# The pooling pairs of a hybrid decoder layer, moved among the merge gate pairs and finished through DRAM

## The chip, the cores and the metric

The kernel runs on one core of one Trainium2 chip. The metric is the device time of one execution in microseconds; the median of several runs is compared. The traces come from the hardware profiler, one execution each.

## The reference

One layer over 1024 positions and 1024 channels. A modulated, normalised input h is projected by one wide matrix w_in. Three causal mixers work on parts of the projection, each is multiplied by its own SiLU gate and projected back, and the three are merged by sigmoid gates:

```python
proj = h @ w_in     # q, k, v, forget | q, k, v, low rank | pu | z_fox, z_gla, z_pool | merge
for g, w in enumerate((2, 4, 8, 16)):            # pooling, 128 channels per group
    lo, hi = g * 128, (g + 1) * 128
    mean = (csum[lo:hi] - lagged_by_w[lo:hi]) / min(count, w)
    diff = mean - pu[..., lo:hi]
    o_pool[..., lo:hi] = (diff @ w_pool[g]) * pool_scale[lo:hi]
y_pool = (o_pool * silu(z_pool)) @ w_br_pool      # y_fox, y_gla alike
merged = sigmoid(m_fox) * y_fox + sigmoid(m_gla) * y_gla + sigmoid(m_pool) * y_pool
out = x + gate * rms_norm(merged @ w_out)
```

All of it is in 32-bit floats.

## The kernel before

Matmuls run on operands split in a high and a low part of a faster float format (`split`, L109: ScalarE writes the high part, VectorE subtracts it for the low part, L110 and L112), three matmuls for one product (`mm3`, L143).

The work goes in stages: start and normalisation, the linear attention (GLA), then the projections for everything else, then the forgetting attention (FoX), the branch projections and the output. The change lies in the stage of projections. There, 256 columns of w_in make one *pair* (`pair`, L900) of two 128-channel output tiles over 1024 positions. `seven` (L843) computes a pair with seven products of 12 matmuls, after Strassen and Winograd. The operands made of h stay in SBUF (`h_combos`, L786, makes the combinations once, on GpSimd and VectorE). The operands made of weights are formed for each pair by `load_seven` (L812): two loads of 512 KB, four additions on GpSimd (S tiles, L825), seven splits. Their tiles rotate over nine slots (`wt`), so a pair's weights can be at most nine products ahead.

PSUM has eight banks under five names; the seven products take them as `("acc", "a", "c", "a", "c", "b", "d")`, with one bank each behind b and d and two behind the others. The sums of products (u, v, p and the outputs, L858, L868, L882) are read out by VectorE, ScalarE and GpSimd with priority. The first output tile of a pair (`small_out`, L947) takes a slot of tag `wh`, which has three, and the second a slot of `wl`, also three. The second of each pair's weight loads takes `wh` too, so that it reuses the slot that the first output tile of the pair two before it has left. When an output half is complete, `fn` runs on it (`silu2`, `tanh_m`), and when both are, `fin` takes the tile on: stored by `to_dram`, or split and stored as two parts by `parts_to_dram` (L930). Two tiles of 1024 columns rotate under `big` (L926), one slot each; the running sums, the high parts and the tiles of `og_parts` (L940, the GLA output times its gate, read back from DRAM) go through these two.

The order in the program is: gate pairs zg0 and zg1, with h_combos between them, then for q = 0, 1 the pairs pu, zp (the pooling input and its gate), fq, fk, zf (FoX queries, keys and gate), then twelve merge gate pairs m, the first four each followed by one `og_parts`, and in the twelfth the first loads and scores of FoX (`start_ahead`). For pooling, `window` (L963) makes the running sums of a group by doubling (one to four steps for widths 2 to 16) and turns the tile of pu into the differences. Both groups' windows stand behind the pair pu, and `fin_pool` stands in the gate pair zp: it splits the differences into parts dh and dl, multiplies them by the group's w_pool in banks b and d (tiles pspl), scales the product by pool_scale and by the gate (L990), splits and stores. For the first group of a pair that comes ahead of the pair's seventh product in the program, for which bank d is needed.

This order isn't that of the chip: a planner with a simulated clock (`schedule_with_timeline_sim=True`) places each engine's instructions, and each SP-issued transfer, by readiness and program order; slots and banks are given out in program order. Each engine and the SP queue then run their list in order, and a wait holds what stands behind it.

Of the kernel before, what the change touches and what calls it, by code (L numbers as in the profile page):

```python
# [29 lines left out]
def kernel(  # L30
# [42 lines left out]
    def halves():  # L73
        return ((0, slice(0, HALF)), (1, slice(HALF, S)))
# [7 lines left out]
    def bank(tag, name, shape=(P, HALF)):  # L82
        if tag == "acc":
            return ps_acc.tile(list(shape), F32, tag="acc", name=name, bufs=2)
        return ps_acc.tile(list(shape), F32, tag=tag, name=name, bufs=BANKS[tag])
# [3 lines left out]
    def spill(name, n):  # L89
        return [dram.tile([P, S], F32, tag=f"{name}{j}", name=f"{name}{j}") for j in range(n)]  # L90
# [5 lines left out]
    fqh_dram, fkh_dram = spill("fqh_d", 4), spill("fkh_d", 4)  # L96
    fql_dram, fkl_dram = spill("fql_d", 4), spill("fkl_d", 4)
    sz_dram, szg_dram, m_dram = spill("sz_d", 4), spill("szg_d", 4), spill("m_d", 24)
    gate_dram = dram.tile([8, P], F32, tag="gate_d", name="gate_d")
    ff_dram = dram.tile([8, S], F32, tag="ff_d", name="ff_d")  # L100
    fc_dram = dram.tile([8, S], F32, tag="fc_d", name="fc_d")
# [7 lines left out]
    def split(raw, hi, lo, scale=1.0, E=None):  # L109
        i = A.activation(hi, raw, AF.Copy, scale=scale)  # L110
        if scale == 1.0:
            j = (E or V).tensor_tensor(out=lo, in0=raw, in1=hi.bitcast(F32), op=ALU.subtract)  # L112
        else:
            j = V.scalar_tensor_tensor(  # L114
                out=lo, in0=raw, scalar=scale, in1=hi.bitcast(F32), op0=ALU.mult, op1=ALU.subtract
            )
        return i, j
# [25 lines left out]
    def mm3(ps, wh, wl, rh, rl, first, last):  # L143
        T.matmul(ps, wh, rh, start=first, stop=False)  # L144
        T.matmul(ps, wh, rl, start=False, stop=False)  # L145
        T.matmul(ps, wl, rh, start=False, stop=last)  # L146
# [753 lines left out]
    def pair(col, name, f, fin, fn=None):  # L900

        o, done = {}, {}

        def dst(j):
            o[j] = big(f"o{j}_{name}") if f is plain else small_out(j, name)
            return o[j]

        def post(j, i, hs):
            if fn is not None:
                with tc.high_priority():  # L910
                    fn(o[j][:, hs], f"{name}{j}{i}")
            done[j] = done.get(j, 0) + 1
            if done[j] == 2:
                fin(j, o[j])

        f(col, name, dst, post)
        return o
# [3 lines left out]
    def to_dram(tiles):  # L921
        return lambda j, t: stores.append(nc.sync.dma_start(tiles[j], t))
# [3 lines left out]
    def big(name, dt=F32):  # L926
        brot[0] += 1
        return sh(GT[brot[0] % 2], name, dt=dt)

    def parts_to_dram(t, hi_d, lo_d, name, scale=1.0, hi=None):  # L930
        if hi is None:
            hi = big(f"hi_{name}", F32R)
        split(t, hi, t.bitcast(F32R), scale)
        nc.sync.dma_start(hi_d, hi.bitcast(F32))
        nc.sync.dma_start(lo_d, t)
# [38 lines left out]
        V.scalar_tensor_tensor(out=u[:, w - 1 : S], in0=cur[:, w - 1 : S], scalar=1.0 / w, in1=u[:, w - 1 : S],  # L974
                               op0=ALU.mult, op1=ALU.subtract)

    def fin_pool(q, d):
        def f(j, t):
            g = 2 * q + j
            raw = cst.tile([P, P], F32, tag="Fd", name=f"wpr{g}", bufs=2)  # L980
            nc.sync.dma_start(raw, w_pool[0, g])
            wph = sp.tile([P, P], F32R, tag="wph", name=f"wph{g}")
            wpl = sp.tile([P, P], F32R, tag="wpl", name=f"wpl{g}")
            split(raw, wph, wpl)
            dh, dl = big(f"dh{g}", F32R), big(f"dl{g}", F32R)
            split(d[j], dh, dl)
            for i, hs in halves():
                ps = bank("bd"[i], f"pspl{g}{i}")
                mm3(ps, wph, wpl, dh[:, hs], dl[:, hs], True, True)
                V.scalar_tensor_tensor(out=t[:, hs], in0=ps, scalar=psc[:, g : g + 1], in1=t[:, hs],  # L990
                                       op0=ALU.mult, op1=ALU.mult)
            parts_to_dram(t, oph_dram[g], opl_dram[g], f"op{g}")
        return f

    pair(C_ZG, "zg0", plain, to_dram(szg_dram[0:2]), silu2)
    h_combos()
    pair(C_ZG + 256, "zg1", seven, to_dram(szg_dram[2:4]), silu2)
    for q in range(2):
        u = pair(C_PU + q * 256, f"pu{q}", seven, lambda j, t: None)
        for j in range(2):  # L1000
            window(2 * q + j, u[j])
        pair(C_ZP + q * 256, f"zp{q}", seven, fin_pool(q, u), silu2)
        pair(C_FQ + q * 256, f"fq{q}", seven, fin_qk(q, fqh_dram, fql_dram, SCL, "q"))
        pair(C_FK + q * 256, f"fk{q}", seven, fin_qk(q, fkh_dram, fkl_dram, 1.0, "k"))
        pair(C_ZF + q * 256, f"zf{q}", seven, to_dram(sz_dram[2 * q : 2 * q + 2]), silu2)
    vf = {}
    hq = {}
    kk = {}
# [77 lines left out]
    def start_ahead():  # L1086
        load_qk(0)
        for i in (7, 6):
            ahead[0, 0, i] = scores(0, 0, i)

    for q in range(12):
        if q == 11:
            hook[0] = start_ahead
            wrot[0] = 3
        pair(C_M + q * 256, f"m{q}", seven, to_dram(m_dram[2 * q : 2 * q + 2]), tanh_m)
        if q < 4:
            og_parts(q)

    tr_stack.close()
    tq_stack.close()  # L1100
# [245 lines left out]
```

## Time and profile before

| what | value |
|---|---|
| runs | 1119.51, 1112.82, 1114.29 us |
| median | 1114.29 us |
| the profiled execution | 1110.77 us, span 1109.0 us, mean granted clock 0.992 |
| stage of the pairs zg1 to zf1 | about 302 to 521 us of the span |
| merge gate pairs | about 521 to 752 us |

The profile counts from the span's start. PE is TensorE's matmuls, PEld its weight loads, DVE VectorE, ACT ScalarE, POOL GpSimd, SP the engine that issues nearly all transfers. A window's row has the stretch, its length, each engine's busy time with its instructions in brackets, TensorE's granted clock as a share of full speed, the busy share of the DMA engines, and GB/s. A row of the timeline has start, duration, engine, line, operation, output and inputs, and in square brackets the idle time before with what ended it.

### The profile page before, as it was taken

What the parts mean: (1) busy time and instruction counts of PE and PEld (TensorE: products, weight loads), DVE (VectorE), ACT (ScalarE), POOL (GpSimd) and SP (SyncE); (2) the same over time, 40 slices, a digit from 0 to 9 for tenths busy, and PEclk for the clock granted to TensorE, in tenths of its full rate; (3) what the DMA queues carried; (4) which work ended last, traced back from release to release, by engine and by line L of the source; (5) the groups of instructions that cost most, each with busy time, mean ns of one, the idle gap of its engine ahead of it and who ended that gap; (6) DMA issues with size and microseconds to landing.
All of it is one profiled execution on the core that took longest, in us unless ns stands there. A gap on an engine that the chain in (4) does not pass through costs nothing.

```text
span 1109.0 us, 15436 instructions
## 1 busy us (share of the span) xinstructions
PE 1058.1 (95%) x5599; PEld 855.0 (77%) x5599; DVE 741.7 (67%) x1403; ACT 462.6 (42%) x877; POOL 384.8 (35%) x339
## 2 busy tenths in 40 slices
PE   5899989999998999899999999999999999999997
PEld 3579779887776888688888888887776776787886
DVE  6638796674898777997656565557675769487323
ACT  6336453443643342343434344435543437343111
POOL 1023152123266145445555444431210434353000
PEclk9999999999999999999999999999999999999999
DMA  9930111202141543156763333359959562464232
GB/s 316 310 106 20 39 40 59 81 25 67 72 128 50 184 142 95 38 198 221 254 200 114 116 124 121 125 154 349 271 184 286 206 173 86 169 221 132 84 106 77
DMA packets 97776, 159.33 MB, mean 144 GB/s; under 512 B 8266, under 2 KB 71324, under 8 KB 97700
## 3 DMA queue, kind: packets, MB, share of 16 engines
q1 hardware_dynamic: 97348, 157.54, 44.5%
q8 instruction: 44, 0.72, 0.3%
q10 hardware_dynamic: 352, 0.80, 0.3%
q14 instruction: 32, 0.26, 0.1%
HBM read 113.16 MB, written 45.16 MB: 143 GB/s over the span
## 4 chain that ended last, share of the span: by engine, by line
PE 68%; DMA 12%; DVE 11%; issue 3%; POOL 3%; ACT 2%; SPq 1%; DVEq 0%; ACTq 0%; POOLq 0%
PE pp_m L146 7%; PE pp_m L144 7%; PE pp_m L145 7%; PE pso L1298 3%; PE pso L1297 3%; PE po L1156 3%; PE pso L1296 3%; PE psy L144 2%; PE psc L655 2%; PE psy L146 2%; PE psy L145 2%; PE tp L1146 2%; DMA kl<-fkl_d 2%; DMA wa<-in_w_ada_dram 1%; PE ps_gv L168 1%
## 5 line engine op out<-in xcount | busy, mean ns | idle before, releaser
L144 PE MATMUL psy<-ogh,wh_y 128*128 128x512 f32 x192 | 75.9, 401 | 6.7 <-DMA ogh<-ogh_d 3.7
L146 PE MATMUL psy<-ogh,wl_y 128*128 128x512 f32 x192 | 74.0, 394 | 1.8 <-DVE wl_y L114 1.8
L145 PE MATMUL psy<-ogl,wh_y 128*128 128x512 f32 x192 | 75.5, 393 | 0.0
L144 PE MATMUL pp_m<-hh,w_m 128*128 128x512 f32 x192 | 74.7, 389 | 0.0
L145 PE MATMUL pp_m<-hl,w_m 128*128 128x512 f32 x192 | 74.7, 389 | 0.0
L146 PE MATMUL pp_m<-hh,w_m 128*128 128x512 f32 x192 | 74.7, 389 | 0.0
L112 DVE TENSOR_TENSOR w_m<-wr_m,w_m 128x512 fp32r<-128x512 f32 x36 | 43.1, 1201 | 44.1 <-ACT w_m L110 44.1
L1052 POOL TENSOR_SCALAR_AFFINE_SELECT Fd<-F 128x128 f32<-128x128 f32 x64 | 22.1, 350 | 127.7 <-DVE mx L1074 89.2
L1081 ACT ACTIVATE t<-t,ng 128x1024 f32<-128x1024 f32 (+3 forms) x64 | 49.6, 776 | 37.3 <-DVE ng L1079 34.7
L112 DVE TENSOR_TENSOR w_m<-S_m,w_m 128x512 fp32r<-128x512 f32 x48 | 57.2, 1221 | 3.1 <-ACT w_m L110 2.3
L566 POOL TENSOR_TENSOR e<-cum 128x256 f32<-128x256 f32 x24 | 17.8, 743 | 108.6 <-DVE kt L570 45.6
L1069 DVE CUSTOM_DVE_ANT_0 t<-psL,F 128x512 f32<-128x512 f32 (+2 forms) x80 | 41.3, 524 | 20.7 <-PE psL L1066 9.0
L793 POOL TENSOR_TENSOR sb<-hh,hl 128x512 f32<-128x512 f32 x16 | 23.1, 1467 | 85.4 <-PE pr L330 65.9
L1297 PE MATMUL pso<-wol,mh 128*128 128x512 f32 (+1 forms) x136 | 51.2, 377 | 0.0
L1296 PE MATMUL pso<-woh,mh 128*128 128x512 f32 (+1 forms) x136 | 51.2, 376 | 0.0
L957 ACT ACTIVATE o_m<-o_m 128x512 f32<-128x512 f32 x48 | 29.0, 628 | 53.1 <-DVE o_m L858 31.7
L1298 PE MATMUL pso<-woh,ml 128*128 128x512 f32 (+1 forms) x136 | 51.0, 376 | 0.0
L1300 DVE TENSOR_TENSOR yo<-pso,gb 128x512 f32<-128x512 f32 (+1 forms) x17 | 11.2, 660 | 55.8 <-ACT jk L1299 55.8
L144 PEld LDWEIGHTS psy<-ogh,wh_y 128*128 128x128 f32 x192 | 36.3, 189 | 15.4 <-DMA ogh<-ogh_d 4.0
L1148 ACT COPY PT<-tp 128x512 f32<-128x512 f32 (+1 forms) x64 | 31.6, 504 | 38.5 <-PE tp L1146 35.3
L1146 PE MATMUL tp<-ident,t 128*128 128x128 f32 x288 | 45.4, 280 | 1.9 <-ACT t L1081 1.1
L1156 PE MATMUL po<-PT,vf 128*64 128x256 f32 (+1 forms) x320 | 45.6, 366 | 0.0
(585 smaller groups left out, 3334.8 us busy)
## 6 DMA issues: line engine op xcount, KB each, us to landing
wa<-in_w_ada_dram SPq DMA_DIRECT2D x24, 512.0 KB, 8.3
wr_m<-in_w_in_dram SPq DMA_DIRECT2D x24, 512.0 KB, 3.7
m_d<-o_m SPq DMA_DIRECT2D x24, 512.0 KB, 2.9
m_in<-m_d SPq DMA_DIRECT2D x24, 512.0 KB, 6.5
xn<-in_x_dram SPq DMA_DIRECT2D x8, 512.0 KB, 6.3
kl<-fkl_d SPq DMA_DIRECT2D x16, 256.0 KB, 9.3
kk<-fkh_d SPq DMA_DIRECT2D x16, 256.0 KB, 10.7
F<-fc_d SPq DMA_DIRECT2D x8, 512.0 KB
```

Source lines behind the costliest of these rows:

```text
L112: j = (E or V).tensor_tensor(out=lo, in0=raw, in1=hi.bitcast(F32), op=ALU.subtract)
L144: T.matmul(ps, wh, rh, start=first, stop=False)
L145: T.matmul(ps, wh, rl, start=False, stop=False)
L146: T.matmul(ps, wl, rh, start=False, stop=last)
L1069: V.tensor_tensor_reduce(out=t[:, c0:e], in0=ps[:, : e - c0], in1=Fb[p, h][:, c0:e], scale=1.0, scalar=-3e38, op0=ALU.subtract, op1=ALU.ma ...
L1081: A.activation(t[:, :W], t[:, :W], AF.Exp, bias=ng[:, 0:1], accum_out=sm)
L1146: T.transpose(tp[:, j, :], t[:, kb * P : (kb + 1) * P], ident)
L1148: A.copy(pts[h, kg][:, 0:nb, qs], tp[:, 0:nb, :])
L1156: T.matmul(po[64 * h : 64 * h + 64, q0:256], vf[p // 2, kb // 4][:, kb % 4, col : col + 64], pts[h, kb // 4][:, kb % 4, q0:256], start=(kb ...
L1296: T.matmul(ps[:, :w], mh[k][:, sl], hi, start=(k == 0), stop=False)
L1297: T.matmul(ps[:, :w], mh[k][:, sl], lo, start=False, stop=False)
L1298: T.matmul(ps[:, :w], ml[k][:, sl], hi, start=False, stop=(k == NK - 1))
```

## The change

The four pooling pairs leave their places ahead of the q pairs. They now stand one by one ahead of the first four merge pairs: pu0, m0, zp0, m1, pu1, m2, zp1, m3. The window of a pair's first group runs when its output tile is complete, the second group's after the following merge pair; the differences are stored to DRAM (`df_dram`). The gate pairs store their SiLU tile (`szp_dram`). The finishing of a group (`pool_parts`) reads both back behind the merge pairs 4 to 7, one group each, in the two rotating tiles, and takes the banks acc and b in place of b and d.

```diff
+    df_dram, szp_dram = spill("df_d", 4), spill("szp_d", 4)
...
-    def fin_pool(q, d):
+    def fin_window(q, late):
         def f(j, t):
             g = 2 * q + j
-            raw = cst.tile([P, P], F32, tag="Fd", name=f"wpr{g}", bufs=2)
-            nc.sync.dma_start(raw, w_pool[0, g])
-            wph = sp.tile([P, P], F32R, tag="wph", name=f"wph{g}")
-            wpl = sp.tile([P, P], F32R, tag="wpl", name=f"wpl{g}")
-            split(raw, wph, wpl)
-            dh, dl = big(f"dh{g}", F32R), big(f"dl{g}", F32R)
-            split(d[j], dh, dl)
-            for i, hs in halves():
-                ps = bank("bd"[i], f"pspl{g}{i}")
-                mm3(ps, wph, wpl, dh[:, hs], dl[:, hs], True, True)
-                V.scalar_tensor_tensor(out=t[:, hs], in0=ps, scalar=psc[:, g : g + 1], in1=t[:, hs],
-                                       op0=ALU.mult, op1=ALU.mult)
-            parts_to_dram(t, oph_dram[g], opl_dram[g], f"op{g}")
+            def run():
+                window(g, t)
+                nc.sync.dma_start(df_dram[g], t)
+            if j == 0:
+                run()
+            else:
+                late.append(run)
         return f
+    def pool_parts(g):
+        raw = cst.tile([P, P], F32, tag="Fd", name=f"wpr{g}", bufs=2)
+        nc.sync.dma_start(raw, w_pool[0, g])
+        wph = sp.tile([P, P], F32R, tag="wph", name=f"wph{g}")
+        wpl = sp.tile([P, P], F32R, tag="wpl", name=f"wpl{g}")
+        split(raw, wph, wpl)
+        d, dh = big(f"d{g}"), big(f"dh{g}", F32R)
+        nc.sync.dma_start(d, df_dram[g])
+        dl = d.bitcast(F32R)
+        split(d, dh, dl)
+        pss = []
+        for i, hs in halves():
+            ps = bank(("acc", "b")[i], f"pspl{g}{i}")
+            mm3(ps, wph, wpl, dh[:, hs], dl[:, hs], True, True)
+            pss.append(ps)
+        t = big(f"zp{g}")
+        nc.sync.dma_start(t, szp_dram[g])
+        for (i, hs), ps in zip(halves(), pss):
+            V.scalar_tensor_tensor(out=t[:, hs], in0=ps, scalar=psc[:, g : g + 1], in1=t[:, hs],
+                                   op0=ALU.mult, op1=ALU.mult)
+        parts_to_dram(t, oph_dram[g], opl_dram[g], f"op{g}")
...
     for q in range(2):
-        u = pair(C_PU + q * 256, f"pu{q}", seven, lambda j, t: None)
-        for j in range(2):
-            window(2 * q + j, u[j])
-        pair(C_ZP + q * 256, f"zp{q}", seven, fin_pool(q, u), silu2)
         pair(C_FQ + q * 256, f"fq{q}", seven, fin_qk(q, fqh_dram, fql_dram, SCL, "q"))
...
+    def pool_pair(q, kind, late):
+        if kind == "u":
+            pair(C_PU + q * 256, f"pu{q}", seven, fin_window(q, late))
+        else:
+            pair(C_ZP + q * 256, f"zp{q}", seven, to_dram(szp_dram[2 * q : 2 * q + 2]), silu2)
...
+    late = []
     for q in range(12):
+        if q < 4:
+            pool_pair(q // 2, "uz"[q % 2], late)
         if q == 11:
             hook[0] = start_ahead
             wrot[0] = 3
         pair(C_M + q * 256, f"m{q}", seven, to_dram(m_dram[2 * q : 2 * q + 2]), tanh_m)
+        if late:
+            late.pop()()
         if q < 4:
             og_parts(q)
+        elif q < 8:
+            pool_parts(q - 4)
```

## Rows read from the trace of the kernel before

**Rows 1.** The page, part 1: busy time, share of the span, instructions.

```profile
PE 1058.1 (95%) x5599; PEld 855.0 (77%) x5599; DVE 741.7 (67%) x1403; ACT 462.6 (42%) x877; POOL 384.8 (35%) x339
```

**Rows 2.** Windows of the two stages: PE, PEld, DVE, ACT, POOL, clock, DMA, GB/s.

```profile
302.00:345.00 43.00, 42.33 (x186) 34.37 (x185) 42.67 (x46) 15.30 (x27) 29.81 (x18) 1.00 0.36 112
345.00:360.00 15.00, 9.95 (x42) 7.29 (x41) 11.79 (x16) 7.36 (x14) 9.03 (x6) 1.00 0.13 36
...
462.00:480.00 18.00, 17.07 (x68) 13.98 (x69) 15.06 (x19) 8.02 (x14) 6.98 (x6) 0.91 0.37 118
480.00:521.00 41.00, 41.00 (x183) 33.94 (x182) 33.03 (x35) 16.68 (x24) 20.23 (x12) 1.00 0.59 205
521.00:736.00 215.00, 214.99 (x948) 177.41 (x947) 133.81 (x143) 89.02 (x152) 113.86 (x72) 1.00 0.46 151
```

**Rows 3.** Windows of PE alone: pooling stage, merge pairs.

```profile
302.00:520.90 218.90, 207.94 (x895) 0.98 0.39 128
520.90:731.00 210.10, 210.09 (x926) 1.00 0.45 148
```

**Rows 4.** Waits of PE, 282 to 521: us in total, times, longest.

```profile
PE pp_zp L144 <- DVE o_zp L990: 3.9, 1, 3.9
PE pspl L144 <- DVE o_zp L858: 3.3, 2, 2.6
PE pspl L144 <- ACT dh L110: 2.5, 1, 2.5
...
PE pspl L145 <- DVE dl L112: 0.5, 1, 0.5
...
PE pp_zg L146 <- DVE w_zg L112: 0.4, 1, 0.4
PE pp_pu L146 <- DVE w_pu L112: 0.3, 1, 0.3
```

**Rows 5.** Windows of 4 us around the two holes, columns as in rows 2.

```profile
358.00:362.00 4.00, 2.21 (x7) 1.80 (x8) 3.56 (x6) 1.79 (x4) 1.91 (x2) 0.82 0.05 16
362.00:366.00 4.00, 4.00 (x15) 3.20 (x14) 3.08 (x4) 1.75 (x4) 0.00 (x0) 0.75 0.91 306
...
460.00:464.00 4.00, 1.38 (x5) 0.88 (x4) 4.00 (x6) 1.72 (x3) 3.48 (x2) 0.87 0.00 0
464.00:468.00 4.00, 4.00 (x14) 3.20 (x13) 3.85 (x7) 0.01 (x1) 0.00 (x0) 0.70 0.37 100
```

**Rows 6.** Window of the instructions on the running sums, DVE alone.

```profile
302.00:521.00 219.00, 31.25 (x32) 0.98 0.39 128
```

**Rows 7.** Timeline of DVE: first sum and last difference of width 8.

```profile
437.50 2.31 DVE L969 TENSOR_TENSOR win<-o_pu 128x1023 f32<-128x1023 f32 x1
...
446.69 1.21 DVE L974 SCALAR_TENSOR_TENSOR o_pu<-win,o_pu 128x1017 f32<-128x1017 f32 x1
```

**Rows 8.** DMA issues: KB each, median us to landing.

```profile
m_d<-o_m SPq DMA_DIRECT2D x24, 512.0 KB, 2.9
...
opl_d<-o_zp SPq DMA_DIRECT2D x4, 512.0 KB, 4.8
```

**Rows 9.** The two parts of the differences: ns min, median, max; first, last start.

```profile
L110 ACT ACTIVATE dh<-o_pu x4: 1044/1050/1062, 342.8 to 470.0; 128x1024 fp32r<-128x1024 f32 x4
L112 DVE TENSOR_TENSOR dl<-o_pu,dh x4: 1210/1222/1227, 344.7 to 478.0; 128x1024 fp32r<-128x1024 f32 x4
```

**Rows 10.** Groups of DVE, 302 to 521: the scaled pooling products.

```profile
L990 DVE SCALAR_TENSOR_TENSOR o_zp<-pspl,colv,o_zp 128x512 f32<-128x512 f32 x8 | 5.7, 748 | 0.6 <-PE pspl L146 0.2
```

**Rows 11.** Timeline of SP: a load of queries for the attention.

```profile
568.68 0.52 SPq L1027 DMA_DIRECT2D hq<-fqh_d  x1
```

**Rows 12.** Timeline of PE's weight loads, 598 to 606.

```profile
603.33 0.19 PEld L146 LDWEIGHTS pp_m<-T2h,w_m 128*128 128x128 f32 x1 [0.33 <-DVE w_m L112]
```

**Rows 13.** Waits of SP's queue, 282 to 755.

```profile
SPq L816 <- DVE dl L112: 20.3, 1, 20.3
```

## The prediction

> **What bounds the kernel now.** I read the busy shares first: PE 95% of the span [rows 1], so a change can gain where PE isn't full, or where its clock is low. The windows come next, cut at the stages. In the merge gate pairs PE is busy 214.99 of 215 us, with DVE at 133.81 [rows 2]: that stretch is bound by PE alone. In the stage before it, which holds the pooling pairs, PE is full in the last 41 us but has holes at 345 to 360 (9.95 of 15 us) and in 462 to 480, while DVE is busy 42.67 of 43 us just ahead of the first hole [rows 2]. So the pooling work overloads DVE, and PE pays for it shortly after.
>
> How much it pays is best counted in matmuls. In the merge pairs 926 of them take 210.1 us, 0.2269 us each; in the pooling stage 895 take 218.9 us [rows 3]. At 0.2269 they would take 203.1, so 15.8 us are lost there. That loss has three parts. Idle PE is 218.9 - 207.94 = 11.0 us [rows 3]. The list of PE's waits says who ended it: the product that waits for a PSUM bank held by a pooling product 3.9, the pooling products for that bank 3.3, for the high part of the differences 2.5, for their low part 0.5, together 10.2; what is left, 0.4 and 0.3, are weights of the pairs around it [rows 4]. Next, the granted clock: behind the two holes it reads 0.82 and 0.75, then 0.87 and 0.70 over 4 us each [rows 5], that is part of the time at the lower of the two levels, 1.2 instead of 2.4 GHz. The missing shares, (0.18 + 0.25 + 0.13 + 0.30) x 4, are 3.4 us of full-speed work. The rest, 1.4 us, are slow first matmuls after each stop.
>
> **The change, part by part.** No matmul is added or dropped: seven products per pair and the 24 pooling matmuls stay. So on PE the sum is only about waits.
>
> Removed: the pooling pairs leave the stretch in which the work of h_combos and of the first gates is still queued on DVE. All of the 15.8 us can go, except the 0.7 of weights at the start, where a pair of q takes the place of a pooling pair and needs its weights just as early. That is -15.1. What was next behind the removed waits is PE itself, as in 480 to 521 [rows 2], where the same q, k and gate pairs run with no hole at 33.03 of 41 us on DVE.
>
> Moved, windows: the running sums and differences cost DVE 31.25 us in 32 instructions [rows 6]. They now fall among eight pairs of 84 x 0.2269 = 19.06 us. A merge pair costs DVE 133.81 / 215 x 19.06 = 11.9 us, so eight of them and the windows want 126 of 152 us, 83%, and some more with the gates' products. The cover is there, but not idle: DVE was about as full as that in 480 to 521, without a PE hole. I cost this at nothing. If the cover fails, the place is this: the first half's tile of a pooling pair stays occupied until the window is done and stored, and the second weight load of the pair after next takes that same slot. The window of width 8 ran from 437.50 to 447.90 [rows 7], begun 3 us after its pair's products ended, and a store lands in 4.8 us at worst [rows 8]: 18 us after the pair, of the 19 that the merge pair between gives. Then load, splitting and subtraction come late by up to 3 us, once for each of two pairs. Bounds 0 to 6, taken 0, because without the neighbouring window of width 16 behind it DVE is less crowded there.
>
> Added, the way through DRAM: eight stores and eight reloads of 512 KB, 8.4 MB, on the same queue. The merge stretch moves 151 GB/s at a DMA share of 0.46; q and k pairs at 205 GB/s and 0.59 had no PE hole [rows 2]. 8.4 MB over eleven pairs, 210 us, add 40 GB/s. I cost bandwidth at nothing. The price is in latency, which I follow for one group: reload of the differences 4.8 (the slowest shown), high part 1.05, low part 1.22 [rows 9], six matmuls 1.36, reload of the gate 4.8, two scaled products 1.5 [rows 10], high and low part again 2.3, store 4.8 [rows 8]: 21.8 us. The two rotating tiles make the four groups a chain, since the next reload takes the slot that the last store leaves. 21.8 against 19.06 per pair means that the groups fall behind by 2.7 us each, four groups some 11 us, and there are four more merge pairs behind them: late, but not at the end of the stage. With the quickest shown, 2.9 us per transfer [rows 8], the chain is 16.1 us and keeps up. The Trainium skill ("DMA: Bandwidth & Descriptors", section "Anatomy of one DMA — SWDGE (gpsimd) path") gives about 2.0 us plus bytes over 436 GB/s, measured on another kind of queue; 512 KB would be 3.2 us, an estimate, and the chain 17.0, which also keeps up and leaves the sum as it is.
>
> Added, waits on PE: the pooling products stand in PE's order where the planner guessed their operands ready, and the matmuls of the next pair stand behind. Today's waits for the two parts, 2.5 and 0.5, stay in kind, so I take 3.0 us for the four groups. The lower bound is 0: the planner can place them late, behind other work. Even less isn't excluded, if they fill gaps of weights; but there are hardly any gaps (0.01 us in 215). The upper bound is the longest wait of today, 3.9, for each of four groups: 15.6. I stay near the low end because the two waits over a bank lose their reason. The scaled product no longer needs the gate's own pair to be through silu; that gate lies in DRAM by then. Bank d isn't used any more, and bank b is free again after matmuls, reload and products, 1.36 + 4.8 + 1.5 = 7.7 us, against 13 us until the next pair's sixth product wants it.
>
> Added, waits on other queues: the gate's reload waits on SP until the pooling matmuls have let its tile go, with the next weight loads behind it; and the scaled product waits on DVE for that reload, with weight splits behind it. Both are the last rival's matter; in the sum they are nothing as long as the planner keeps the order.
>
> The sum: -15.8 + 0.7 + 3.0 = -12.1 against the profiled 1110.77, 1098.7 us. The median of the shown runs lies 3.5 above the profiled one, so I expect 1102.
>
> **The rivals.** *All of it comes back.* The pooling products find their operands ready and PE never waits: -15.1 or a little more, 1099. For it: the merge pairs ran through the multiplication of the linear attention's gate, a chain of the same kind through DRAM, without a single wait, and the planner moves loads far ahead (loads of q for the attention stand at 568.68, long before their pair [rows 11]). Against it: the four pooling products are the very place where PE waited.
>
> *The stall moves along.* DVE at 83% on average is full in bursts, and splits for weights and for differences stand in one queue. Then the 10.2 us of waits recur with their clock and restarts, 4.8, and nothing is left: -15.1 + 15 = 0, 1114. For it: weights in the merge pairs come just in time, one weight load into PE waited 0.33 us for a split on DVE [rows 12]. Against: today the bursts come on top of h_combos' leftovers, afterwards they don't.
>
> *A reload blocks the weights: slower.* A load of weights has stood behind a wait on SP for 20.3 us here, until DVE had made a low part [rows 13]. After the change each of the four gate reloads waits on SP for its pooling matmuls, and since the weights have no slack [rows 12], what SP loses PE loses soon after. It decides from 15.1 / 4 = 3.8 us per group; at 8 us, about the time the bank is held, it costs 32, so +17: 1131. The Trainium skill states as a rule of DMAs, on the same page and section, that "any semaphore wait happens on the issuing sequencer before dispatch"; by that rule this happens whenever the planner's order is wrong by more than the slack, and the 20.3 us agree with it. Against: the order is planned with the same waits in it, and today's fill of SP with waiting stores, in 480 to 521, cost PE nothing.
>
> *The change doesn't do what it says.* The planner issues by readiness, not by place in the program. If it pulls the finishing of groups forward to the last pooling pairs, it lands where the windows load DVE most, some 5 us of waits: 1105.
>
> **How the numbers follow.** Forecast (1099.5 to 1107) 0.45; all back 0.22; the stall moves along 0.22; slower 0.08; not as said 0.03. One per cent of 1114.29 is 11.1 us, about what a measurement of this kernel can tell from no change, so faster begins at 1103.1. The forecast lies astride it, somewhat over half on the fast side: 0.28 + 0.22 make 0.50 for faster. Same takes 0.17 + 0.21 + 0.03 = 0.41, slower 0.09. The range: down to 1096, which is all back on a run 2 us below the median; up to 1114, which holds the pooling waits' upper bound, -15.1 + 15.6. Outside lie the blocked reloads, part of the stall that moves along, and little below, under 2 in 10.
>
> **What would show it.** The stage of q, k and gates from 302 on without a PE hole and with clock 1.00; no wait of a pooling product or of a seventh product for a scaled product; in the merge stretch PE waits of the pooling products of about 3 us in all, for high or low parts; SP's waits over the weights not longer than now. I am wrong if PE's list of waits names weights or their loads in the merge pairs (windows or SP too late), if the granted clock falls there, or if DVE is found full while PE waits.

## The result and the profile after

The forecast was 1102 us, 1096 to 1114. The changed kernel took 1126.45 us in the median of four runs (1124.15 to 1133.44), beside 1115.53 for the kernel before: a ratio of 1.0103, 95% interval 1.007 to 1.0137. Run again later on another occasion (e15 below) the ratio was 1.0096 (1.0066 to 1.0126). So it is slower by 1%, some 11 us, and outside the range on the slow side. The profiled execution took 1126.96 us, 16.2 more than the profiled one of before. Up to line 97 the numbers of both kernels agree; L109 to L112 of before are L110 to L113 now, L143 to L146 are L144 to L147, `load_seven`'s L816 is L817, the sums' L858 is L859.

The busy shares first; they answer to [rows 1]. PE is busy 10.7 us longer with the same 5599 matmuls, which already says that part of the loss is clock and not idle time.

```profile
PE 1068.8 (95%) x5599; PEld 862.4 (77%) x5599; DVE 748.3 (67%) x1403; ACT 463.3 (41%) x877; POOL 389.1 (35%) x339
```

The windows of after, columns as in [rows 2]. The q, k and gate pairs now end near 440, the merge pairs with the pooling pairs among them follow.

```profile
345.00:360.00 15.00, 15.00 (x68) 12.43 (x67) 12.04 (x12) 6.69 (x11) 9.17 (x6) 1.00 0.41 149
...
460.00:480.00 20.00, 17.51 (x75) 13.38 (x74) 14.24 (x15) 6.75 (x12) 12.13 (x7) 1.00 0.48 160
480.00:500.00 20.00, 14.93 (x55) 10.97 (x54) 13.06 (x13) 7.40 (x13) 10.65 (x6) 0.88 0.68 236
500.00:520.00 20.00, 20.00 (x78) 16.23 (x77) 14.93 (x19) 8.23 (x15) 7.50 (x6) 0.86 0.33 106
...
580.00:600.00 20.00, 16.66 (x69) 13.01 (x68) 13.47 (x15) 6.98 (x11) 8.45 (x5) 0.94 0.47 166
600.00:640.00 40.00, 37.46 (x155) 29.96 (x154) 25.99 (x28) 17.03 (x30) 21.05 (x14) 0.94 0.43 146
640.00:660.00 20.00, 16.56 (x61) 13.11 (x61) 13.05 (x17) 8.63 (x14) 8.42 (x6) 0.83 0.52 173
660.00:768.00 108.00, 108.00 (x480) 89.48 (x479) 69.56 (x89) 43.59 (x73) 45.73 (x33) 1.00 0.57 178
```

The hole of before at 345 to 360 is closed: 15.00 of 15 us. New holes lie at 460 to 500 and 580 to 660; from 480 to 520 and from 580 to 660 the clock reads 0.83 to 0.94. The same in matmuls, as for [rows 3], with PE alone:

```profile
302.00:440.00 138.00, 137.31 (x605) 1.00 0.42 143
440.00:767.80 327.80, 310.92 (x1314) 0.96 0.49 162
```

At 0.2269 us, 605 matmuls need 137.3 us: up to 440 only 0.7 us are lost, as much as the weights that the prediction left in. The 1314 behind need 298.1 of 327.8 us, so 29.7 us are lost: 16.9 idle (327.8 - 310.92), and 12.8 in busy time that is longer than at full clock. Who ended the idle time, as in [rows 4], for 282 to 770:

```profile
PE pp_m L145 <- ACT w_m L111: 5.6, 2, 3.3
PE pspl L145 <- ACT dh L111: 3.4, 1, 3.4
PE pp_m L147 <- DVE w_m L113: 2.8, 2, 2.5
PE pspl L145 <- DVE o_m L859: 2.4, 1, 2.4
PE pp_zp L145 <- ACT w_zp L111: 1.9, 1, 1.9
...
PE pp_zp L147 <- DVE w_zp L113: 0.5, 1, 0.5
```

Weights (w_m, w_zp) make 10.8 us, pooling products (pspl) 5.8. The weights come first, so the next view is the list of SP, which loads them. First the timeline of SP at the first two holes (PE stood still before 468.28 and before 491.15), then its waits in 455 to 492, as in [rows 13]:

```profile
457.99 0.34 SPq L985 DMA_DIRECT2D df_d<-o_pu  x1
460.56 0.34 SPq L943 DMA_DIRECT2D og_in<-og_d  x1
461.01 0.67 SPq L817 DMA_DIRECT2D wr_zp<-in_w_in_dram  x1
...
481.04 0.32 SPq L936 DMA_DIRECT2D ogl_d<-szg  x1
481.45 0.41 SPq L943 DMA_DIRECT2D og_in<-og_d  x1
...
484.27 0.32 SPq L944 DMA_DIRECT2D szg<-szg_d  x1
484.69 0.43 SPq L817 DMA_DIRECT2D wr_m<-in_w_in_dram  x1
```

```profile
SPq L985 <- DVE win L969: 10.8, 1, 10.8
SPq L817 <- POOL S_zp L826: 7.7, 1, 7.7
SPq L935 <- ACT og_in L111: 4.9, 1, 4.9
...
SPq L943 <- DVE win L970: 2.2, 1, 2.2
```

Two things stand ahead of the weights there. At 461.01 it is the window: the second load of the gate pair zp0 takes the slot that the first pooling tile holds until its window is done and its store issued; the store waited 10.8 us in SP's list for work of the window. Between that store and the load stands a reload of `og_parts` (460.56), which waited 2.2 us more for the tile of the second window. In e14 below, without it, the load follows the store by 0.5 us (458.60 and 459.10) and this hole is gone. At 484.69 it is the linear attention's `og_parts`: its stores and reloads, each with a wait of its own in the two rotating tiles, stand one by one ahead of a load of m1. The Trainium skill says, on the page "DMA: Bandwidth & Descriptors", section "Anatomy of one DMA — SWDGE (gpsimd) path", that a semaphore wait is taken on the issuing sequencer before dispatch; the rows agree, a transfer that waits holds all that is queued behind it.

Ahead of the third hole (PE stood still before 597.99) the longest wait belongs to a new store: the gates of zp1 wait 11.0 us on SP for the last step of their SiLU (L955), two stores of `og_parts` follow, and only then the load of weights (SP's waits in 575 to 592, then its timeline).

```profile
SPq L923 <- DVE o_zp L955: 12.6, 2, 11.0
```

```profile
587.05 2.37 SPq L923 DMA_DIRECT2D szp_d<-o_zp  x2
...
591.54 0.77 SPq L817 DMA_DIRECT2D wr_m<-in_w_in_dram  x1
```

On DVE the two windows of the first pooling pair run back to back in 452.76 to 461.9, although the second is called one merge pair later in the program. A selection of the timeline:

```profile
452.76 2.31 DVE L970 TENSOR_TENSOR win<-o_pu 128x1023 f32<-128x1023 f32 x1
...
460.61 1.21 DVE L975 SCALAR_TENSOR_TENSOR o_pu<-win,o_pu 128x1021 f32<-128x1021 f32 x1
...
461.81 0.68 DVE L859 TENSOR_TENSOR o_m<-pp_m,p_m 128x512 f32<-128x512 f32 x1
...
468.26 1.21 DVE L113 TENSOR_TENSOR w_zp<-wr_zp,w_zp 128x512 fp32r<-128x512 f32 x1 [3.85 <-ACT w_zp L111]
469.39 0.68 DVE L859 TENSOR_TENSOR v_m<-pp_m,u_m 128x512 f32<-128x512 f32 x1
471.31 4.04 DVE L113 TENSOR_TENSOR w_zp<-S_zp,w_zp 128x512 fp32r<-128x512 f32 x2 [1.25 <-ACT w_zp L111]
```

### The profile page after: what moved, and what is told of

It reads as the page before. It is cut to its first block, busy times and chain, and to the rows that moved or that the text cites. A ratio compares the mean times of both kernels' runs of the same rounds, so it can differ in the third digit from the quotient of the medians.

```text
span 1125.2 us, 15447 instructions
## 1 busy us (share of the span) xinstructions
PE 1068.8 (95%) x5599; PEld 862.4 (77%) x5599; DVE 748.3 (67%) x1403; ACT 463.3 (41%) x877; POOL 389.1 (35%) x339
## 2 busy tenths in 40 slices
DMA packets 100080, 167.72 MB, mean 149 GB/s; under 512 B 8522, under 2 KB 71580, under 8 KB 100004
## 4 chain that ended last, share of the span: by engine, by line
PE 61%; DMA 13%; DVE 12%; POOL 6%; issue 4%; ACT 3%; SPq 1%; DVEq 0%; ACTq 0%; POOLq 0%
PE pp_m L147 4%; PE pp_m L145 4%; PE pp_m L146 4%; PE po L1186 4%; PE psy L145 3%; PE psy L147 3%; PE tp L1176 3%; PE psy L146 3%; PE pso L1328 3%; PE pso L1327 3%; DMA wr_m<-in_w_in_dram 3%; PE pso L1326 3%; PE psc L656 2%; PE psL L1088 1%; PE ps_gv L169 1%
## 5 line engine op out<-in xcount | busy, mean ns | idle before, releaser
L145 PE MATMUL pp_m<-hh,w_m 128*128 128x512 f32 x192 | 77.6, 404 | 5.6 <-ACT w_m L111 5.6
L147 PE MATMUL pp_m<-hh,w_m 128*128 128x512 f32 x192 | 77.3, 403 | 0.3 <-DVE w_m L113 0.3
L146 PE MATMUL pp_m<-hl,w_m 128*128 128x512 f32 x192 | 77.0, 401 | 0.0
L147 PE MATMUL psy<-ogh,wl_y 128*128 128x512 f32 x192 | 74.9, 399 | 1.8 <-DVE wl_y L115 1.8
L146 PE MATMUL psy<-ogl,wh_y 128*128 128x512 f32 x192 | 76.3, 397 | 0.0
L113 DVE TENSOR_TENSOR w_m<-S_m,w_m 128x512 fp32r<-128x512 f32 x48 | 57.3, 1230 | 1.6 <-ACT w_m L111 1.6
L113 DVE TENSOR_TENSOR w_m<-wr_m,w_m 128x512 fp32r<-128x512 f32 x36 | 40.1, 1116 | 24.0 <-ACT w_m L111 24.0
L145 PEld LDWEIGHTS pp_m<-hh,w_m 128*128 128x128 f32 x192 | 37.7, 197 | 14.3 <-ACT w_m L111 6.5
```

## The experiments

Ratios are to the kernel before on the same chip, with the 95% interval; "us" is the difference of ratios times 1113. The changed kernel stands at +11.1 us (mean of 1.0103 and 1.0096). Executions of one kernel spread by 6 to 9 us here (1113.56 to 1120.15 in e1), so single ones are not compared by time, and differences under 2 to 3 us are not read.

| run | what | ratio | us |
|---|---|---|---|
| e15 | changed kernel again | 1.0096 (1.0066 to 1.0126) | +10.7 |
| e1 | pooling tile out of tag wh | 1.0038 (1.002 to 1.0056) | +4.2 |
| e2 | no windows | 0.9981 (0.9958 to 1.0004) | -2.1 |
| e3 | no finishing | 1.0039 (1.0012 to 1.0066) | +4.3 |
| e4 | pooling pairs at their old place | 1.0108 (1.0071 to 1.0144) | +12.0 |
| e7, e16 | og_parts early | 1.0003 (0.9975 to 1.0031), 1.0026 (1.0002 to 1.0049) | +1.6 |
| e14 | og_parts late | 1.0072 (1.0045 to 1.01) | +8.0 |
| e5, e17 | e1 and e7 together | 0.9999 (0.9974 to 1.0025), 1.0001 (0.9977 to 1.0026) | 0.0 |
| e6 | e5, products one pair later | 0.9995 (0.9963 to 1.0027) | -0.6 |
| e8 | e5, differences in a tile of their own | 0.9988 (0.997 to 1.0007) | -1.3 |
| e9 | e8, gates too | 0.9968 (0.9952 to 0.9985) | -3.6 |
| e12 | e9, second window kept behind the merge pair | 0.9971 (0.9952 to 0.9989) | -3.2 |
| e10 | e9, no windows | 0.9902 (0.9882 to 0.9923) | -10.9 |
| e13 | kernel before, no windows | 0.9897 (0.9856 to 0.9938) | -11.5 |

**First round: slot, windows, finishing, DRAM.** e1 lets go of the slot, e2 drops the windows, e3 the finishing, e4 keeps the way through DRAM but puts the four pairs ahead of the q pairs again.

```diff
# e1
-        return wtile(("wh", "wl")[j], f"o{j}_{name}", F32, (P, S))
+        return wtile("wl" if name[:2] == "pu" else ("wh", "wl")[j], f"o{j}_{name}", F32, (P, S))
# e2
-                window(g, t)
# e3, in pool_parts: w_pool, reload of the differences, split, 24 matmuls, scaled products go
-        nc.sync.dma_start(d, df_dram[g])
...
-        split(d, dh, dl)
...
-            mm3(ps, wph, wpl, dh[:, hs], dl[:, hs], True, True)
...
# e4 (the calls of pool_pair and late ahead of and behind the merge pairs go)
     for q in range(2):
+        pool_pair(q, "u", late)
+        pool_pair(q, "z", late)
+        late.pop()()
         pair(C_FQ + q * 256, ...)
```

> One part undone: the first output tile of a pooling input pair takes a slot of the tag wl, which has room, in place of wh, so that no second weight load waits for a window and its store. PE's list of instructions stays the same. Theory A (the held slot delays weight loads, and the pairs behind inherit the delay): the holes before the first pooling gate pair (2.4 us) and in the merge pair behind it (5.1 us) go, with most of the low clock at 480 to 520, and so does part of the hole at 598: 8 to 14 us less than the changed kernel, near 1114. Theory B (the windows' block of work on VectorE delays the reading out of products and the weight splits, whoever holds the slot): no change within 3 us, 1124 to 1129. Theory C (the finishing behind the merge pairs costs the time): no change either.

> Leaves out the windows: the pooling input itself is stored in place of the differences; all else stays. A and B together: 10 to 18 us less than the changed kernel. If A alone holds, no more than 2 us below the run with the other slot; if B holds, clearly below it (5 us or more). C: within 3 us of the changed kernel.

> Leaves out the finishing's reload of the differences, their two parts, the 24 pooling matmuls and the scaled products; the gate alone is read back, split and stored. The matmuls alone are 24 x 0.227 = 5.4 us. Theory C: the holes at 623 and 646 (5.8 us) and the low clock behind them go as well, 13 to 17 us less than the changed kernel. A or B: 5 to 8 us less, the holes at 468 to 500 and 598 stay.

> The way through DRAM alone: the pooling pairs stand at their old place ahead of the q pairs, differences and gates go to DRAM, and the groups are finished behind merge pairs 4 to 7 as in the change. If the place among the merge pairs is what costs (A or B there), the merge pairs show only the finishing's holes: 1106 to 1117. If the finishing costs (C), holes of about 6 us with low clock appear in the merge pairs: 1113 to 1122. If the windows cost wherever they stand: as the changed kernel, 1122 to 1130.

Freeing the slot takes back 6.9 us, and the hole before 468 is gone; PE's waits for w_m stay, 5.5 and 1.5:

```profile
PE pp_m L147 <- DVE w_m L113: 5.5, 3, 2.6
PE pspl L145 <- ACT dh L111: 2.7, 1, 2.7
...
PE pp_m L145 <- ACT w_m L111: 1.5, 1, 1.5
```

Leaving the windows out takes back 13.2, more than the whole loss. Leaving the finishing out takes back 6.8, of which its 24 matmuls at 0.2269 are 5.4 in themselves; the holes at 467 to 498 and near 600 stay in it. In e4 the first hole of before doesn't come back. Where the second was, one stop of 2.0 us is left, at 450, for weights of a q pair, with VectorE busy 19.96 us from 440 to 460. The longest waits lie among the merge pairs: 3.5 us for weights before 535.19, behind stores of a gate and of `og_parts` on SP, and 3.3 for a bank before 619.59. The time is as long as the changed kernel's, so for the time as a whole the place of the four pairs decides little here. The two versions share the late finishing and the way through DRAM among the merge pairs, with what stands there already, and they share the windows too: 1122 to 1130 was named as the sign that the windows cost wherever they stand, and e4 took 1123.9. Neither the finishing alone nor the slot alone is all of it.

**Second round: the og_parts.** What e1 left was a load of weights behind `og_parts` in SP's list. e7 calls them at the end of each round of q, k and gate pairs instead of behind the first four merge pairs; e5 does that on top of e1; e6 moves the pooling products of e5 one merge pair on.

```diff
# e7, and e5 on top of e1
         pair(C_ZF + q * 256, f"zf{q}", seven, to_dram(sz_dram[2 * q : 2 * q + 2]), silu2)
+        og_parts(2 * q)
+        og_parts(2 * q + 1)
...
-        if q < 4:
-            og_parts(q)
-        elif q < 8:
+        if 4 <= q < 8:
# e6, on top of e5: pool_parts stops after the splits and returns the rest
+        if rest:
+            rest.pop()()
+        if 4 <= q < 8:
+            rest.append(pool_parts(q - 4))
```

> The run with the other slot, and the four finishing steps of the linear attention moved from behind merge pairs 0 to 3 into the q and k pairs ahead. Theory D (their reloads stand in SP's and GpSimd's lists ahead of weight loads and weight sums, now that they fall among the pooling pairs): the holes of the run with the other slot at 490 to 494 (4.0 us) and at 590 to 596 (3.0 us) go, with the low clock behind them: 6 to 10 us less than that run, some 3 us below before. Theory B (the windows' block on VectorE and its late weight splits are the rest): those holes stay, no change within 3 us of the run with the other slot. A new cost is possible for both: the q and k pairs have splits and stores of their own.

> The kernel before this one in the list, and the pooling matmuls, gate reload and scaled products placed one merge pair later in the program than the reload and split of the differences, so that their operands are ready. If the waits of the pooling products (0.8, 2.7 and 0.8 us in the run with the other slot) are a cost of their own: they go, 4 to 7 us less than the kernel before it in the list. If PE's list is bound elsewhere (splits on VectorE late), the waits turn up at other matmuls and the time stays within 3 us.

> The changed kernel with the linear attention's finishing moved ahead alone; the pooling pairs' first output tile holds its slot as in the change. If the held slot and the reloads' place are two separate costs: 6 to 10 us less than the changed kernel and 7 us more than the kernel with both edits. If the held slot's holes come only together with the reloads (the store of the tile stands behind them on SP), then the same time as with both edits within 3 us.

e5 takes back all 11 us and stands level with the kernel before. PE's waits of e5 name one weight wait over 1 us, and two of pooling products:

```profile
PE pspl L145 <- ACT dh L111: 3.4, 1, 3.4
PE pspl L145 <- DVE o_m L859: 1.7, 1, 1.7
PE pp_zp L145 <- ACT w_zp L111: 1.7, 1, 1.7
```

e7 alone, with the slot still held, did nearly as well, 1.6 us above e5 where e1 alone gave back 6.9. e6 gained nothing: its pooling product waited 3.7 us for the high part as before. So that wait is not a product placed too early; its operand comes late. That the chain of the two rotating tiles makes it late is a guess at this point, which the next round tests.

**Third round: the rotating tiles, and the windows again.** e8 reloads the differences into a tile of tag wl, e9 the gates too, so that no group waits for the store of the group before. e10 drops the windows from e9.

```diff
# e8
-        d, dh = big(f"d{g}"), big(f"dh{g}", F32R)
+        d, dh = wtile("wl", f"d{g}", F32, (P, S)), big(f"dh{g}", F32R)
# e9, on top of e8
-        t = big(f"zp{g}")
+        t = wtile("wl", f"zp{g}", F32, (P, S))
```

> The run with the other slot and the early GLA finishing, with the reloaded differences in a slot of the tag wl in place of one of the two rotating tiles, so that this reload no longer waits for the store of the group before. If the pooling products wait on PE (1.7, 3.4 and 0.6 us in that run) because the two rotating tiles chain the groups: the 3.4 and most of the rest go with their low clock, 4 to 8 us less than that run, 1105 to 1109 on the scale of before at 1112. If they wait because ScalarE's and VectorE's lists are late anyway: within 3 us of that run.

> As the kernel ahead of this one, and the reloaded gate in a slot of wl as well, so that this reload no longer waits on SP for the pooling matmuls, nor VectorE for the reload (17.5 us in four waits in the run with the early GLA finishing). If a reload that blocks SP and VectorE delays the weights: another 2 to 5 us less. If these waits are covered (no hole of PE names weights behind them): the same as the kernel ahead within 2 us.

> As the kernel ahead of this one, with the windows left out (the pooling input itself goes on). What the windows cost where nothing else is in the way: if VectorE's cover holds, as was predicted, within 2 us of the kernel ahead; if their block delays the splits of weights and the reading out of products (holes at 456 and 472 in the run with the early GLA finishing, 3 us and some low clock), 4 to 7 us less.

e8 brought 1.3 us and not the 4 to 8 forecast for a broken chain. e9 is the best kernel here that does all the work: 1109.94 us beside 1112.66, 0.32% (0.15 to 0.48) under the kernel before. In its timeline of SP both reloads of a group are issued together with a weight load (in three groups of four; for one the second waits 4.6 us), where the changed kernel's waited one behind the other:

```profile
624.52 0.38 SPq L817 DMA_DIRECT2D wr_m<-in_w_in_dram  x1
625.00 0.46 SPq L1000 DMA_DIRECT2D d<-df_d  x1
625.55 0.38 SPq L1009 DMA_DIRECT2D zp<-szp_d  x1
```

PE's waits for the high part don't go with the chain: they still add up to 3.5 us in e9, in three pieces of at most 1.8. What is gone there is the wait for a bank behind o_m, and every stretch of 10 us from 440 to 740 has a clock of 1.00.

And e10 meets the forecast, 1102.57, but without the windows: in their new place they cost 7.3 us (some 4 to 10 by the two intervals) with every other cause out of the way. That was costed at nothing. Where they cost it is seen in windows of PE alone, e9 first, then e10:

```profile
440.00:520.00 80.00, 77.52 (x337) 1.00 0.42 145
520.00:600.00 80.00, 80.00 (x355) 1.00 0.33 112
600.00:660.00 60.00, 56.92 (x249) 1.00 0.58 196
```

```profile
440.00:520.00 80.00, 79.16 (x350) 1.00 0.43 146
520.00:600.00 80.00, 80.00 (x355) 1.00 0.39 131
600.00:660.00 60.00, 60.00 (x267) 1.00 0.55 186
```

Of the 31 matmuls that e9 is behind up to 660, 13 are lost where the windows of the first pooling pair run (widths 2 and 4), none where those of the second run (8 and 16, the longer ones, from 530 to 554), and 18 at the finished groups, where no window runs any more.

**Fourth round: where the windows cost.** e12 keeps the second group's first copy, and with it all of that window but its first sum, behind the latest read-out of the following merge pair on VectorE; e13 takes the windows out of the kernel before.

```diff
# e12, in window
+            i = V.tensor_copy(nx[:, 0:sh], cur[:, 0:sh])
+            if g % 2 and sh == 1:
+                after(i, newest[0])
# e13
-        for j in range(2):
-            window(2 * q + j, u[j])
```

> Both own tiles, as in the run before, and of each pooling pair the second group's window is kept in VectorE's list behind the last read-out of the following merge pair; all work stays. In the version without this order VectorE ran both windows of a pair back to back, and leaving them out brought 7.4 us. If it is the block that costs, that both windows together stand ahead of a read-out, then the second half of the block moves away and 2 to 5 us come back: ratio 0.992 to 0.995 to the kernel before. If it is the sum of VectorE's work, wherever it stands, the time stays within 2 us of the version without the order, ratio about 0.997. If the window now stands ahead of the weights' subtractions of the next pairs instead, TensorE waits for low parts and it is slower, above 1.000.

> The kernel before with the running sums and differences left out, so that the pooling products get the raw projections; everything else stays in its old place. It measures how much of the 15.8 us that the pooling stage lost belongs to the windows. If the holes there come from the windows' 31 us on VectorE, as the prediction said, 10 to 15 us come back: ratio 0.987 to 0.991. If they come from the banks that the pooling products and their scaled products hold, which stay, no more than 5 us come back: ratio above 0.995. Compared with the changed kernel without windows, 13.5 us quicker than with them, it says whether the windows cost more or less in the new place than in the old one.

In e12 the second windows did move, from 464.97 to 482.21 and from 540.43 to 554.29, except for their first sums of 1.2 us (465.50 and 543.40), and the time stayed. That speaks for their work as the cost, wherever it stands among these pairs, and against the block of two. The loss was not the same one, though: the trace of e12 has 327 matmuls from 440 to 520 and 262 from 600 to 660, so more is lost at the windows and less at the finished groups, with about the same sum. e13 shows what it cost before: the window of PE alone that [rows 3] has with 895 matmuls now holds 962.

```profile
302.00:520.90 218.90, 218.17 (x962) 1.00 0.42 144
```

67 more at 0.2269 are 15.2 us in that stage, of which 11.5 remain in the whole kernel.

**Fifth round: which of slot and og_parts.** e14 puts `og_parts` behind the merge pairs 8 to 11; the changed kernel, e7 and e5 are measured side by side once more (no edit).

```diff
# e14
-        if q < 4:
-            og_parts(q)
-        elif q < 8:
+        if 4 <= q < 8:
             pool_parts(q - 4)
+        elif q >= 8:
+            og_parts(q - 8)
```

> The four og_parts of the linear attention stand behind the merge pairs 8 to 11, after the pooling groups, where they stood behind the merge pairs 0 to 3; everything else as changed, the slot of tag wh too. If the loss comes from their reloads and stores standing in SP's list among the pooling pairs, ahead of weight loads, it goes as it did when they were put into the stage of q and k: ratio 0.998 to 1.002. If it went there only because that stage had something to hide them in, and they now hold up weights or the last finished group at the end of the stage instead, the ratio stays at 1.007 or above. The wait of SP's list for a store of og parts between 475 and 490 is gone in either case.

> The changed kernel itself once more, beside the two that follow, for a narrower interval: four runs stood behind 1.0103, and the executions of one kernel spread by several microseconds here. If the loss is what it seemed, the ratio is 1.008 to 1.012; if the four runs lay high by chance, 1.004 to 1.007, and the slot and the og_parts, 7 and 11 us by the first runs, overlap less than it seemed.

> The og_parts in the stage of q and k, the slot still held, once more: its profiled execution was the longest of its ten. If the held slot and the og_parts make the same weights late, so that one of them is enough, this stays at 0.998 to 1.002, within 2 us of the next run. If the slot has a cost of its own, this is slower than the next run by 3 us or more.

> Both undone, slot and og_parts, once more beside the two before: ratio 0.998 to 1.002 if the first runs were right. Its distance to the run before is the slot's own cost once the og_parts are out: under 2 us if the two overlap, about 7 us if they add.

e14 missed the ratio that I had set for the theory and met the one of its rival, that `og_parts` need a stretch to hide in. It still shows the mechanism: with the slot held as in the changed kernel, PE is full where the first holes were (first fence), and the loss turns up elsewhere, as the first of PE's waits (second fence).

```profile
460.00:480.00 20.00, 20.00 (x90) 1.00 0.51 172
480.00:500.00 20.00, 20.00 (x89) 1.00 0.31 106
```

```profile
PE psL L1088 <- DMA kk<-fkh_d: 5.7, 1, 5.7
PE pspl L145 <- DVE o_m L859: 3.4, 1, 3.4
```

Now the first keys of the FoX attention (kk) come late, behind the same transfers, at a stretch where the DMA share is 0.68 to 0.72. So `og_parts` cost time among the pooling pairs, and at the end too. e15 confirmed the 1%. e16 against e17 gives the slot 2.8 us without `og_parts` (first runs 0.4, mean 1.6, each uncertain by some 3), against 6.9 with them: the two overlap for the most part. The first hole shows it best: it is gone when either of the two goes (e1, e14; from 460 to 480 PE is busy for 20.00 us in both). I read from this that the weights tolerate one delay of a few microseconds and not two.

## Why the prediction was wrong

**Right.** The loss in the pooling stage was sized well and its cause too. 15.8 us were read, 0.7 left in: in the changed kernel the stretch up to 440 loses 0.7 us, and e13, which removes the windows alone, gains 15.2 us of matmuls there. Bandwidth is no cause: 167.72 MB instead of 159.33, and e10 with all this traffic runs at 1102.57. The chain of a group was put at 21.8 us; the reloads that follow the first were issued at 640.60, 662.51 and 685.55, 21.9 and 23.0 apart. That this fits so well is partly luck: in the first of these the reload of the gate came 11.3 us after that of the differences, where 8.4 were summed, and the next group 10.6 us later, where 13.4 were.

**The step that failed: "I cost this at nothing", for the moved windows.** It rested on DVE at 83% on average and on 480 to 521, where DVE was as full without a hole. The same work of 31 us cost 11.5 us in the old place (e13, 6.9 to 16.0) and 13.2 in the new one (e2); with slot, `og_parts` and tiles put right it still costs 7.3 (e9 against e10). So of the 11.5 us that hung on the windows only some 4 were to be had by moving them among these pairs, and e9 with its 3.6 has got about that. An average share doesn't say whether there is cover: a window takes 5 to 10 us on the engine (452.76 to 457.97 for width 2, [rows 7] for width 8) through which the weights' low parts and most read-outs pass in order. But a full VectorE isn't enough for a hole either: from 540 to 560 the changed kernel has it busy for 19.86 of 20 us, with PE full, and in e9 more than half of the cost lies behind the windows, not at them. Taken together, the windows at 7 us would have turned the forecast into about 1109.

**Its second part: the slot, "bounds 0 to 6, taken 0".** The place was named correctly, and the arithmetic gave 3 us for each of two pairs. Alone it measured 6.9 (e1). It was taken as 0 because DVE would be less crowded without the width 16 window behind. But the planner ran both windows back to back anyway. The sum also held 4.8 us until the store lands, which the slot doesn't wait for (0.5 us from store to load in e14), and left out the reload of `og_parts` that stands between the two.

**"Nothing as long as the planner keeps the order", for SP's queue.** This looked at the gates' reloads waiting for the pooling matmuls. Those waits were 0.8 and 0.2 us. What stood ahead of the weights were the new stores, which the prediction did not follow on SP (10.8 us for the differences of the first group, 11.0 for the gates of zp1), and work that the change does not touch in the diff's core: `og_parts`, whose place in the program is the same loop, but whose neighbours had become pooling pairs. Moving it away gave back 9.5 us of the 11.1 (e7 and e16). Every step of the loop into which work is moved should have been followed through SP's list, the old steps and the new stores as well as the new reloads.

**Pooling products, 3.0 (0 to 15.6).** 5.8 us of PE's waits, inside the bounds. Half of the reason was wrong: the wait over a bank did not go, it became one for bank b behind a read-out of the merge pair (o_m, 2.4). "Late, but not at the end of the stage" left out that a late group stops PE: it waited 3.4 us for a high part. Tiles of their own gave 3.6 us (e5 to e9, by the two intervals some 1 to 6), though these waits stayed in sum; what they gave is shown, by which way is not.

**Clock and restarts were left out of all new waits.** The old holes had cost 11.0 us idle and 4.8 behind them; the new ones cost 16.9 idle and 12.8 behind them. With what was measured the sum is -15.1 + 10.8 (weights) + 5.8 (products) + 12.8 (clock and restarts) = +14.3, and the profiled executions differ by 16.2; most of the rest, 1.6 us, are seven matmuls more in the stage's records (1917 beside 1910 up to its end).

**The rivals.** "A reload blocks the weights" was right in kind, a transfer's wait on SP ahead of weight loads, with the wrong transfer and too high a price. "The stall moves along" (1114) has the time of e5, level with before once slot and `og_parts` are put right; that it comes about as the rival said, by bursts on VectorE alone, is not shown.

**Open.** Why the windows still cost 7.3 us in e9 is not settled. Moving most of the second windows (e12) moved the loss and didn't lessen it. PE's waits for the high parts of the differences are 3.5 us in e9 and 0.5 in e10, but not because the differences reach DRAM late: in e9 the last of their stores was issued at 553.88 and the first reload at 602.35. Leaving the windows out also changes the lists that the planner makes for all engines, and no run separates this from VectorE's time.

## What to carry to other kernels

Before moving work, write down for the stretch that receives it each transfer in the queue's order with its wait, also of steps that stay: a load that has no slack behind a step with a wait was most of the loss. Leaving the suspected work out of the *old* kernel measures the most that a move of it can bring (here 11.5 us) before anything is rebuilt, and leaving it out of the new one what it costs there (13.2 at first, 7.3 with the rest put right). And a wait of PE is to be booked at more than its length when the clock falls behind it: here 16.9 us of waits became 29.7.

## What the runs showed of the hardware

Short stops cost clock, but not each of them. In the changed kernel stops of 3.3 and 3.4 us (before 597.99 and 646.37), and stops of 2.3 and 2.5 us 8 us apart (before 491.15 and 499.42), gave stretches of 20 us at a mean granted clock of 0.83 to 0.89, a part of them at 1.2 instead of 2.4 GHz: the 4 us behind 500, 600 and 648 read 0.50. Single stops of 1.9 and 2.4 us (before 468.28 and 623.15) left it at 1.00. In all it was 12.8 us of longer busy time for 16.9 us of idle time, against 4.8 for 11.0 before.

The same subtraction on VectorE takes 0.69 us or 1.2 and more. In the timeline of after the split of one 128x512 tile took 0.69 us at 463.71, with GpSimd idle, and 1.21 at 468.26 while GpSimd worked on another addition (467.64 to 468.91), and the pair at 471.31 took 4.04 for two beside GpSimd's multiplication of 2.86. An addition with one input in PSUM took 0.68 at 469.39, with GpSimd adding at the same time (469.00, 1.62 us):

```profile
467.64 1.27 POOL L826 TENSOR_TENSOR S_zp<-wr_zp,wr_zp 128x512 f32<-128x512 f32 x1 [11.42 <-DMA wr_zp<-in_w_in_dram]
469.00 1.62 POOL L826 TENSOR_TENSOR S_zp<-S_zp,wr_zp 128x512 f32<-128x512 f32 x1
...
471.95 2.86 POOL L945 TENSOR_TENSOR szg<-szg,og_in 128x1024 f32<-128x1024 f32 x1
```

If this holds throughout, VectorE is slowest just when GpSimd forms the weights' sums late, and a backlog of the two would feed itself. No run here took the two apart; it is read from these rows alone.
